# Branch C: the later score stages of one unit placed beside the first score stages of the next unit

## The chip, the cores and the metric

The kernel runs on one core of a Trainium2 chip. The metric is the device time of one execution in microseconds (us); the time of a version is the median over its runs. A core has engines that run side by side, each with its own queue of instructions that it works off in order: the tensor engine (PE; the loading of its weights is listed apart, as PEld), the vector engine (DVE), the scalar engine (ACT), the GpSimd engine (POOL) and the engine whose queue here only starts transfers (SP). They wait for one another through semaphores. Matrix products land in PSUM, in banks of 512 float32 for each of 128 partitions.

## The reference, cut to what matters

One layer of a decoder trunk on 2048 positions with 1024 features. One projection feeds three causal mixers; their gated outputs are joined, multiplied by `w_out`, added to the residual, and normalised:

```python
h = jnp.einsum('bsd,de->bse', x, w_in)
a_u, a_v, a_g, b_val, b_glu, b_g, c_q, c_f, c_i, c_g = jnp.split(h, offsets, axis=-1)
y_a = _sgu_mixer(a_u, a_v, ...) * silu(a_g)          # A: gating over chunks of 128 positions
y_b = _conv_module(b_val, b_glu, ...) * silu(b_g)    # B: causal convolution of width 31
y_c = _hgrn2_mixer(c_q, c_f, c_i, ...) * silu(c_g)   # C: linear recurrence, 4 heads of 128
x = layernorm(ALPHA * x + concat(y_a, y_b, y_c) @ w_out)
```

The change touches branch C alone. Its mixer works on chunks of 64 positions, with `f = lb + (1-lb)*sigmoid(c_f)`, `k = 1-f` and `q = silu(c_q)`:

```python
b = jnp.cumsum(log_f, axis=2)
decay = jnp.exp(jnp.where(causal, b[:, :, :, None, :] - b[:, :, None, :, :], -inf))
scores = jnp.einsum('bhtd,bhsd,bhtsd->bhts', qc, kc, decay)
o_intra = jnp.einsum('bhts,bhsv->bhtv', scores, vc)
o_inter = jnp.einsum('bhtd,bhdv->bhtv', qc * jnp.exp(b), state)
new_state = exp(b_last) * state + einsum('bhsd,bhsv->bhdv', kc * exp(b_last - b), vc)
o = o * rsqrt(mean(o*o) + eps) * norm_g
```

Everything is float32.

## The kernel before, in words

The 2048 positions are four groups of 512, two groups to a half. Each half runs branch B's projections, in the first half branch A as well, then branch C's values, and then eight *units* of branch C: four heads, each with the two groups of the half. After both halves comes the product with `w_out`, and the normalisation. In the profile shown below the eight units of the first half are executed from 219 to 365 us, those of the second half from 519 to 730 us, each with the work left over at its end.

A product of two float32 matrices is written as three matrix instructions (`three`, L200 to L203): each factor is split into a high and a low part, and high by high, high by low and low by high are summed. One such instruction has a 128x128 weight tile and 512 columns. They make up most of the tensor engine's time, and here they are called **stream matmuls**. A unit (`hgrn_unit`, L357 to L583) has three projections of 24 stream matmuls each: `pm_f` (the gate f), `pm_q` (the query) and `pm_cg` (the output gate). Everything else that the unit does on the tensor engine is small work between stream matmuls, its own or those of the next unit:

- stage 0 (L405): 16 matmuls with weight tiles 128x32 and 80 columns, the scores within blocks of 4 positions
- stage 1 (L405): 16 matmuls, 128x32 and 48 columns, blocks of 16
- stage 2 (L440): 8 matmuls, 128x64 and 96 columns, blocks of 64
- the chunk halves (`chunk_halves`, L500): 4 matmuls, 128x64 and 64 columns, blocks of 128
- `transposes` (pk, L515), `states` (pst, L531: four matmuls; after each the vector engine folds the result into the running state, s, L535/L537), `outputs` (po, L549/L553: two matmuls for each of four chunks) and `finish` (pt, L571)

A group of such small matmuls is called a **burst** here. The profile counts each small float32 matmul as two instructions (x32 for 16 of them).

Between the stages the vector engine masks the scores into ST (by way of a buffer S32 for stages 0 and 1, L417 and L423) and prepares the next stage's operand: X1, then X4, X16 and Q64, with the products of f kept in T, and K overwritten stage by stage. ACT copies S32 and the chunk halves into ST (L433, L503), makes KT from pk (L518), takes the squares of the outputs (jk, L558), and applies the sigmoid and silu (f L362, X L369, sg L582). sigmoid, and the others, need different function tables, so that ACT has a table load at changes between them (ACT_TABLE_LOAD).

**What sets the order.** The program counts a virtual clock: each group of three stream matmuls advances it by 0.64 (`tick`, L186). A step of a unit is put into a queue with a due time (`later(dt, fn)`, L182) and is issued at the first tick that reaches it. The distances are the constants in one line: DST0 (unit's projections of f and q to stage 0) 4.5, DST (from each score stage to the next) 5.5, DKT 2.5, DPST 2.0, DPO 2.5, DPT 6.0. So stage 0 of a unit falls near the end of its `pm_cg`, and the later stages fall into the next two units' projections. The compiler's scheduler then places the instructions on each engine; only the small matmuls are kept in their mutual program order (`pinned`), and everything else may move by its dependencies.

Buffers that bear on the order: the projections share three PSUM banks, the score stages two (`sc`), pst, po and the pair pk/pt one each (`st`, `o`, `tr`); K has two buffers, X1, X4, X16 and Q64 one each, sg two, and S32 is one buffer for all units.

Of the kernel before, what the change touches and what calls it, by code (L numbers as in the profile page):

```python
# [27 lines left out]
GPH = NG // NHALF  # L28
# [15 lines left out]
NWARM = 9  # L44
FIRST = ("00", "x0", "x1", "10", "x2", "01", "x3", "x4", "11", "x5", "x6", "x7")
DTAP, DNORM, DWO = (1.5, 1.35), 8.0, 2.5
DST0, DST, DKT, DPST, DPO, DPT = 4.5, 5.5, 2.5, 2.0, 2.5, 6.0


def _masks():  # L50
# [34 lines left out]
def _body(tc, nc, d, ctx):  # L85
    from contextlib import ExitStack

    def pool(name, bufs=1, space=None, stack=ctx, **kw):
        if space is not None:
            kw["space"] = space  # L90
        return stack.enter_context(tc.tile_pool(name=name, bufs=bufs, **kw))
# [90 lines left out]
    def later(dt, fn):  # L182
        heapq.heappush(queue, (clock[0] + dt, order[0], fn))
        order[0] += 1
# [169 lines left out]
                    tick(0.64)  # L354
                nc.scalar.copy(vh[:, gi * 4 + tt, :], pt)  # L355

    def hgrn_unit(h, g, gi, w, x, pl, vh, ST, S32):  # L357
        nm = f"{h}_{g}"
        wf_, wq, wg = w
        pf = proj_f(wf_, x, f"f{nm}")  # L360
# [15 lines left out]
        def tb(ap, *shape):  # L376
            return ap.unsqueeze(len(ap.shape)).to_broadcast(shape)

        def prep(st):
# [6 lines left out]
            else:  # L386
                nc.vector.tensor_mul(X[:, :, 2:6:3, :], X[:, :, 4:7:2, :],
                                     tb(T[:, :, 1:3], P, n, 2, b))
                nc.vector.tensor_mul(X[:, :, 3, :], X[:, :, 5, :], tb(T[:, :, 1], P, n, b))

        def stage(st):
            b = 4 ** st
            n = G // (4 * b)
            nsc = 10 if st == 0 else 6
# [89 lines left out]
            cur["X"], cur["T"] = X, T  # L484
            if st < 2:
                prep(st + 1)
                later(DST, lambda: stage(st + 1))
            else:
                later(DST, chunk_halves)

        def chunk_halves():
            X, T = cur["X"], cur["T"]
# [158 lines left out]
    def getx(g):  # L651
        if g not in xg:
            xg[g] = load_x(g)
        return xg[g]
# [81 lines left out]
    vh = vhp.tile([P, GPH * 4, 512], F32, name="vh")  # L736
# [9 lines left out]
    for hf in range(NHALF):  # L746
        last = hf == NHALF - 1
# [6 lines left out]
        xs = [getx(hf * GPH + gi) for gi in range(GPH)]  # L754
        if hf == 0:
# [3 lines left out]
            with ExitStack() as esw:  # L759
                wo_start(pool("wos", stack=esw, reuse_waits="tile"))  # L760
                with ExitStack() as esa:
                    pl = pool(f"a{hf}", stack=esa, reuse_waits="tile")
# [8 lines left out]
        pl = pool(f"c{hf}", stack=esc, reuse_waits="tile")  # L771
        STs = []
# [4 lines left out]
        S32 = pl.tile([P, 4, 32], F32, name=f"S32{hf}")  # L777
        nc.gpsimd.memset(S32, 0.0)
        u = 0
        for h in range(4):  # L780
            w = [load_wf(o + h, hf) for o in (C_F, C_Q, C_G)]
            for gi in range(GPH):
                hgrn_unit(h, hf * GPH + gi, gi, w, xs[gi], pl, vh, STs[u % 2], S32)
                u += 1
                if h == 3 and gi == 0 and not last:
                    getx(hf * GPH + gi + GPH)
# [83 lines left out]
    with ExitStack() as esa:  # L870
        pl = pool("a1", stack=esa, side="right", reuse_waits="tile")
# [177 lines left out]
```

## Time and profile before

| | |
|---|---|
| median of 3 runs | 933.75 us (932.08 to 935.57) |
| the profiled execution's own time | 934.35 us |
| its span (first to last instruction) | 932.6 us |
| PE matmul busy | 906.8 us, 97% of the span |
| DVE busy | 714.4 us, 77% |
| ACT busy | 392.9 us, 42% |
| POOL busy | 82.1 us, 9% |
| granted TensorE clock, mean | 0.996 |

Busy time of PE is modelled at its ends, and instructions overlap there: two matmuls that start 0.23 us apart are listed with 0.39 us each. What an instruction costs is therefore read from the distance between the starts of its neighbours and not from its listed duration. A row of the timeline gives the start in us, the listed duration, the engine, the line, the operation, output and inputs, the shape, and how many instructions were taken together. Where an engine stood idle before the row, the end of the row names the idle time and what ended it.

### The profile page before, as it was taken

What the parts mean: (1) busy time and instruction counts of PE and PEld (TensorE: products, weight loads), DVE (VectorE), ACT (ScalarE), POOL (GpSimd) and SP (SyncE); (2) the same over time, 40 slices, a digit from 0 to 9 for tenths busy, and PEclk for the clock granted to TensorE, in tenths of its full rate; (3) what the DMA queues carried; (4) which work ended last, traced back from release to release, by engine and by line L of the source; (5) the groups of instructions that cost most, each with busy time, mean ns of one, the idle gap of its engine ahead of it and who ended that gap; (6) DMA issues with size and microseconds to landing.
All of it is one profiled execution on the core that took longest, in us unless ns stands there. A gap on an engine that the chain in (4) does not pass through costs nothing.

```text
span 932.6 us, 15037 instructions
## 1 busy us (share of the span) xinstructions
PE 906.8 (97%) x5673; PEld 735.1 (79%) x5673; DVE 714.4 (77%) x1614; ACT 392.9 (42%) x774; POOL 82.1 (9%) x127
## 2 busy tenths in 40 slices
PE   9999998999999999999999999999999999999996
PEld 6889886787777777788888877777788887888885
DVE  5998889935787768997999767778785144888777
ACT  6524455143345346634314344443553342543350
POOL 0001100000000000101000000001012000221122
PEclk9999999999999999999999999999999999999998
DMA  7516786121112103511202111111151498455422
GB/s 261 180 35 233 251 301 232 46 91 35 34 35 79 35 13 120 165 66 58 68 1 91 45 46 47 47 46 46 50 167 58 145 351 294 159 171 186 139 91 90
DMA packets 60808, 107.43 MB, mean 115 GB/s; under 512 B 5312, under 2 KB 21952, under 8 KB 60608
## 3 DMA queue, kind: packets, MB, share of 16 engines
q1 hardware_dynamic: 60736, 106.48, 33.6%
q8 instruction: 44, 0.72, 0.3%
q14 instruction: 28, 0.23, 0.1%
HBM read 75.00 MB, written 31.46 MB: 114 GB/s over the span
## 4 chain that ended last, share of the span: by engine, by line
PE 65%; DVE 17%; DMA 6%; ACT 4%; issue 4%; POOL 2%; SPq 0%; POOLq 0%; DVEq 0%; ACTq 0%
DVE acc L285 5%; PE pm_q L201 3%; PE poz L201 3%; PE pm_ci L203 3%; PE pm_ci L201 3%; PE pm_ci L202 3%; PE poz L203 3%; PE poz L202 3%; PE pm_q L203 3%; PE pm_q L202 3%; PE pm_f L201 3%; PE pm_f L203 2%; PE pm_f L202 2%; PE pm_cg L201 2%; PE pm_cg L203 2%
## 5 line engine op out<-in xcount | busy, mean ns | idle before, releaser
L285 DVE SCALAR_TENSOR_TENSOR acc<-bh,vec,acc 128x512 f32<-128x512 f32 x240 | 172.2, 752 | 2.6
L148 DVE TENSOR_TENSOR wl<-rw,wh 128x512 fp32r<-128x512 f32 x84 | 56.8, 688 | 25.8 <-ACT wh L147 25.6
L147 ACT CAST wh<-rw 128x512 fp32r<-128x512 f32 x84 | 49.9, 619 | 40.4 <-PE pm_f L202 11.1
L558 ACT ACTIVATE jk<-po 128x128 f32<-128x128 f32 x64 | 17.8, 278 | 58.5 <-PE po L553 57.6
L201 PE MATMUL pm_f<-xhix,wh 128*128 128x512 f32 x96 | 41.1, 429 | 0.0
L201 PE MATMUL pm_q<-xhix,wh 128*128 128x512 f32 x96 | 41.0, 427 | 0.0
L201 PE MATMUL pm_cg<-xhix,wh 128*128 128x512 f32 x96 | 39.0, 407 | 0.0
L202 PE MATMUL pm_q<-xlox,wh 128*128 128x512 f32 x96 | 39.0, 406 | 0.0
L203 PE MATMUL pm_f<-xhix,wl 128*128 128x512 f32 x96 | 37.8, 393 | 0.0
L203 PE MATMUL pm_q<-xhix,wl 128*128 128x512 f32 x96 | 37.8, 393 | 0.0
L202 PE MATMUL pm_f<-xlox,wh 128*128 128x512 f32 x96 | 37.6, 392 | 0.0
L203 PE MATMUL pm_cg<-xhix,wl 128*128 128x512 f32 x96 | 37.6, 391 | 0.0
L202 PE MATMUL pm_cg<-xlox,wh 128*128 128x512 f32 x96 | 37.5, 390 | 0.0
L201 PE MATMUL pm_ci<-wh_ci,xhix 128*128 128x512 f32 x96 | 37.3, 389 | 0.0
L202 PE MATMUL pm_ci<-wl_ci,xhix 128*128 128x512 f32 x96 | 37.3, 389 | 0.0
L203 PE MATMUL pm_ci<-wh_ci,xlox 128*128 128x512 f32 x96 | 37.3, 389 | 0.0
L227 POOL TENSOR_SCALAR crs<-ss 128x4 f32<-128x4 f32 x16 | 4.6, 286 | 371.0 <-ACT jk L558 371.0
L355 ACT COPY vh<-pm_ci 128x512 f32<-128x512 f32 x16 | 9.4, 589 | 58.1 <-PE pm_ci L203 58.1
L446 DVE COPY_PREDICATED ST<-msk,sc 64x192 f32<-64x192 int32 (+2 forms) x96 | 28.7, 299 | 4.9 <-PE sc L440 2.6
L537 DVE SCALAR_TENSOR_TENSOR s<-s,Tc,pst 128x128 f32<-128x128 f32 x56 | 19.4, 346 | 16.1 <-PE pst L531 15.9
L531 PEld LDWEIGHTS pst<-vh,KT 128*128 128x128 f32 x120 | 19.4, 188 | 14.5 <-DVE s L537 10.4
L503 ACT COPY ST<-sc 64x128 f32<-64x128 f32 x32 | 8.4, 261 | 50.9 <-PE sc L500 50.7
(355 smaller groups left out, 2772.0 us busy)
## 6 DMA issues: line engine op xcount, KB each, us to landing
rw<-wf SPq DMA_DIRECT2D x84, 256.0 KB, 3.1
wob<-wo_dr SPq DMA_DIRECT2D x14, 1024.0 KB, 11.5
xr<-x SPq DMA_DIRECT2D x16, 512.0 KB, 3.9
ry<-y_dr SPq DMA_DIRECT2D x32, 256.0 KB, 2.7
out<-xr SPq DMA_DIRECT2D x15, 512.0 KB, 2.6
wo_dr<-wsh SPq DMA_DIRECT2D x28, 256.0 KB, 3.3
wo_dr<-wsl SPq DMA_DIRECT2D x28, 256.0 KB, 2.8
rx<-xT SPq DMA_DIRECT2D x24, 256.0 KB, 3.4
```

The costliest lines, as they stand in the source:

```text
L147: nc.scalar.copy(hi, src)
L148: nc.vector.tensor_sub(lo, src, hi.bitcast(F32))
L201: nc.tensor.matmul(out, wh, xh, start=first, stop=False, **kw)
L202: nc.tensor.matmul(out, wh, xl, start=False, stop=False, **kw)
L203: nc.tensor.matmul(out, wl, xh, start=False, stop=last, **kw)
L285: nc.vector.scalar_tensor_tensor(a, h[:, k : k + G], vcol(cw + k), a, ALU.mult, ALU.add)
L355: nc.scalar.copy(vh[:, gi * 4 + tt, :], pt)
L446: nc.vector.copy_predicated(ST[rr, :, 64 * m + j0 * b : 64 * m + (j0 + nj) * b], msk[rr, mo : mo + mw].unsqueeze(1).to_broadcast([64, 4, mw]),
L503: nc.scalar.copy(ST[0:64, e:4:2, 64:128], pcv[64 * e : 64 * e + 64])
L531: pinned(nc.tensor.matmul(pst[:, cs], KT_[:, cs], V[:, c, :], start=True, stop=True))
L537: nc.vector.scalar_tensor_tensor(ns, stt[-1], Tc[:, c : c + 1], pst[:, cs], ALU.mult, ALU.add)
L558: nc.scalar.activation(jk, po[:, c * P : (c + 1) * P], AF.Square, accum_out=ss[:, c : c + 1])
```

## The change

A new constant DSTH = 7.7 and a dictionary `held` are added, and each unit is told whether it is the last of its half (`u == 7`). After stage 0, stage 1 is due 7.7 later instead of 5.5. Stage 2 and the chunk halves are not put into the queue at all: they are kept in `held`, and the next unit takes them out. Its stage 0 first runs the stage 2 of the unit before; its stage 1 first runs the chunk halves of the unit before. The last unit of a half keeps the old distances for its own steps. Everything that follows the chunk halves (pk, pst, po, pt) keeps its distance to them.

```diff
-DST0, DST, DKT, DPST, DPO, DPT = 4.5, 5.5, 2.5, 2.0, 2.5, 6.0
+DST0, DST, DSTH, DKT, DPST, DPO, DPT = 4.5, 5.5, 7.7, 2.5, 2.0, 2.5, 6.0
...
+    held = {}
+
+    def hgrn_unit(h, g, gi, w, x, pl, vh, ST, S32, last):
...
+        def then(st, fn):
+            if last:
+                later(DST, fn)
+            elif st == 1:
+                later(DSTH, fn)
+            else:
+                held[st - 2] = fn
+
         def stage(st):
+            if st < 2 and st in held:
+                held.pop(st)()
             b = 4 ** st
...
             if st < 2:
                 prep(st + 1)
-                later(DST, lambda: stage(st + 1))
+                then(st + 1, lambda: stage(st + 1))
             else:
-                later(DST, chunk_halves)
+                then(3, chunk_halves)
...
-                hgrn_unit(h, hf * GPH + gi, gi, w, xs[gi], pl, vh, STs[u % 2], S32)
+                hgrn_unit(h, hf * GPH + gi, gi, w, xs[gi], pl, vh, STs[u % 2], S32, u == 7)
```

From the second of these places on, the line numbers are 3 to 13 higher in the changed kernel: L405 becomes L418, L440 L453, L500 L513, L515 L528, L531 L544, L571 L584, and L582 L595.

How the instructions stand on the engines: in the names, the two numbers after sc, pk, pst and the like are head and group, so that `1_1` is one unit of the first half and `2_0` the next one; `sc` has the stage as third number, 3 being the chunk halves. The first place is the tensor engine, from the `pm_cg` of unit 2_0 to the states of unit 1_1. Before:

```order
L440 MATMUL sc1_1_2_2965<-X16_1_1_2872,K1_1_2541 64x96 x8
...
L405 MATMUL sc2_0_0_3006<-X12_0_2952,K2_0_2841 32x80 x16
...
L571 MATMUL pt1_0_3045<-ident_91,os1_0_2944 128x128 x4
...
L500 MATMUL sc1_1_3_3058<-Q64_1_1_2980,K1_1_2541 64x64 x4
...
L515 MATMUL pk1_1_3081<-ident_91,K1_1_2541 128x128 x4
...
L405 MATMUL sc2_0_1_3100<-X4_2_0_3027,K2_0_2841 32x48 x16
...
L531 MATMUL pst1_1_3142<-vh_113,KT1_1_3086 128x128
```

And in the changed kernel:

```order
L453 MATMUL sc1_1_2_2958<-X16_1_1_2877,K1_1_2516 64x96 x8
L418 MATMUL sc2_0_0_2981<-X12_0_2907,K2_0_2816 32x80 x16
...
L562 MATMUL po1_0_3020<-vh_113,ST0_0_1843 128x128 x2
...
L584 MATMUL pt1_0_3081<-ident_91,os1_0_3040 128x128 x4
...
L513 MATMUL sc1_1_3_3094<-Q64_1_1_2973,K1_1_2516 64x64 x4
L418 MATMUL sc2_0_1_3105<-X4_2_0_3002,K2_0_2816 32x48 x16
...
L528 MATMUL pk1_1_3160<-ident_91,K1_1_2516 128x128 x4
...
L544 MATMUL pst1_1_3179<-vh_113,KT1_1_3165 128x128
```

Stream matmuls stand at each "...". Stage 2 of unit 1_1 and stage 0 of unit 2_0, which had 18 stream matmuls between them, are neighbours, and so are the chunk halves of 1_1 and stage 1 of 2_0. The pk of unit 1_1 now stands 12 stream matmuls behind the second pair, 3 into the `pm_cg` of unit 2_1, and its first pst 12 further on; the pt of unit 1_0 stands 9 stream matmuls into the `pm_q` of unit 2_1, where it stood 3 into `pm_f`. In each half 14 pairs come about in this way, 28 in all, and no pair has a stream matmul between its parts.

The second place is the vector engine around the states of unit 1_1 (s, four instructions), before:

```order
L423 COPY_PREDICATED S320_1847<-msk_97,sc2_0_1_3100 128x8x4
L364 TENSOR_SCALAR f2_1_3091<-f2_1_3091,oml_106,lb_105 128x512
L537 SCALAR_TENSOR_TENSOR s1_1_0_3144<-s1_0_3_2901,Tc1_1_3067,pst1_1_3142 128x128
L365 TENSOR_SCALAR K2_1_3093<-f2_1_3091 128x512
L148 TENSOR_TENSOR wl_27_0_3306<-rw27_0_1_3311,wh_27_0_3305 128x512
L537 SCALAR_TENSOR_TENSOR s1_1_1_3147<-s1_1_0_3144,Tc1_1_3067,pst1_1_3142 128x128
...
L371 TENSOR_TENSOR X12_1_3196<-X12_1_3196,f2_1_3091 128x128x2
```

And in the changed kernel:

```order
L436 COPY_PREDICATED S320_1847<-msk_97,sc2_0_1_3105 128x8x4
L368 TENSOR_SCALAR K2_1_3068<-f2_1_3066 128x512
L374 TENSOR_TENSOR X12_1_3150<-X12_1_3150,f2_1_3066 128x128x2
L375 TENSOR_TENSOR X12_1_3150<-X12_1_3150,f2_1_3066 128x128x2
L470 COPY X4_2_1_3245<-X12_1_3150 128x32x2 x2
L387 TENSOR_TENSOR X12_1_3150<-X12_1_3150,f2_1_3066 128x128x2
L388 TENSOR_TENSOR X12_1_3150<-X12_1_3150,f2_1_3066 128x128
L482 TENSOR_TENSOR f2_1_3066<-f2_1_3066 128x128
L550 SCALAR_TENSOR_TENSOR s1_1_0_3181<-s1_0_3_2947,Tc1_1_3103,pst1_1_3179 128x128
L471 TENSOR_TENSOR X4_2_1_3245<-X12_1_3150,f2_1_3066 128x32x2x3 x2
L550 SCALAR_TENSOR_TENSOR s1_1_1_3184<-s1_1_0_3181,Tc1_1_3103,pst1_1_3179 128x128
```

The four s of unit 1_1 stood ahead of the preparation of X1 for unit 2_1; now the first of them stands behind six rows of that preparation.

The third place is ACT over the same stretch, before:

```order
L503 COPY ST0_1_1845<-sc1_1_3_3058 64x2x64 x2
L582 ACTIVATE sg2_0_3039<-pm_cg2_0_2958 128x512
L518 COPY KT1_1_3086<-pk1_1_3081 128x512
L147 CAST wh_27_0_3305<-rw27_0_0_3307 128x512
L362 ACT_TABLE_LOAD
L362 ACTIVATE f2_1_3091<-pm_f2_1_3041 128x512
...
L433 COPY ST0_0_1843<-S320_1847 32x4x32 x4
...
L369 ACTIVATE X12_1_3196<-pm_q2_1_3096 128x128x4
```

And in the changed kernel:

```order
L365 ACT_TABLE_LOAD
L365 ACTIVATE f2_1_3066<-pm_f2_1_3016 128x512
L147 CAST wh_27_0_3279<-rw27_0_1_3285 128x512
L516 COPY ST0_1_1845<-sc1_1_3_3094 64x2x64 x2
L446 COPY ST0_0_1843<-S320_1847 32x4x32
L595 ACT_TABLE_LOAD
L595 ACTIVATE sg2_0_3014<-pm_cg2_0_2913 128x512
L446 COPY ST0_0_1843<-S320_1847 32x4x32 x3
L372 ACTIVATE X12_1_3150<-pm_q2_1_3071 128x128x4
L531 COPY KT1_1_3165<-pk1_1_3160 128x512
```

Between the chunk halves' copy and the X1 of the next unit ACT now has a copy out of S32, a table load, the sg of unit 2_0, and three more copies, and KT follows X1 where it stood ahead of f. It stands so only in units during which weights are cast; elsewhere the four copies out of S32 stand together.

More of the change, by code (lines that the diff above doesn't have):

```diff
@@ L355, in values @@
                 nc.scalar.copy(vh[:, gi * 4 + tt, :], pt)
-    def hgrn_unit(h, g, gi, w, x, pl, vh, ST, S32):
+    held = {}
+    def hgrn_unit(h, g, gi, w, x, pl, vh, ST, S32, last):
         nm = f"{h}_{g}"
```

## The prediction

> **What bounds the kernel now.** I read the page first: busy time, and the chain that ended last.
>
> ```profile
> span 932.6 us, 15037 instructions
> PE 906.8 (97%) x5673; PEld 735.1 (79%) x5673; DVE 714.4 (77%) x1614; ACT 392.9 (42%) x774; POOL 82.1 (9%) x127
> PE 65%; DVE 17%; DMA 6%; ACT 4%; issue 4%; POOL 2%; SPq 0%; POOLq 0%; DVEq 0%; ACTq 0%
> ```
>
> The tensor engine is busy for 97% of the span. The chain runs through other engines for a third of the span, but they lead it only where a late operand happens to be the last thing that PE asked for. So the time is the sum of PE's steps plus the short waits between them, and the change can act in two ways: on the price of a step between two kinds of matmul, and on waits for a late operand. I then read a long piece of the second half's units by window (busy time and count of PE, PEld, DVE, ACT, POOL; granted clock; DMA share; GB/s).
>
> ```profile
> 502.00:628.00 126.00, 125.77 (x982) 99.69 (x980) 93.55 (x293) 55.23 (x123) 6.57 (x10) 1.00 0.17 57
> ```
>
> DVE is at 74% and ACT at 44% while PE has hardly a gap: both have slack on average, not at every place. The clock is 1.00, so it is no term.
>
> **The price of a burst.** The timeline of PE, at stage 2 of one unit and, 18 stream matmuls later, stage 0 of the next, the pair that the change puts together:
>
> ```profile
> 603.56 0.39 PE L202 MATMUL pm_cg<-xlox,wh 128*128 128x512 f32 x1
> 603.79 0.39 PE L203 MATMUL pm_cg<-xhix,wl 128*128 128x512 f32 x1
> 604.11 0.88 PE L440 MATMUL sc<-X,K 128*64 128x96 f32 x16
> 604.91 0.50 PE L201 MATMUL pm_cg<-xhix,wh 128*128 128x512 f32 x1
> 605.25 0.40 PE L202 MATMUL pm_cg<-xlox,wh 128*128 128x512 f32 x1
> ...
> 608.90 0.39 PE L203 MATMUL pm_cg<-xhix,wl 128*128 128x512 f32 x1
> 609.22 0.76 PE L405 MATMUL sc<-X,K 128*32 128x80 f32 x32
> 609.91 0.50 PE L201 MATMUL pm_f<-xhix,wh 128*128 128x512 f32 x1
> ```
>
> A stream matmul follows another after 0.23 (603.56 to 603.79). The step from a stream matmul into a burst is 0.32 (603.79 to 604.11; 608.90 to 609.22): 0.09 too much. The burst itself, up to the start of the next stream matmul, is 0.80 and 0.69. The step after that first stream matmul is again slow, 0.34 (604.91 to 605.25): 0.11 too much. What a merged pair costs turns on one step that this kernel never makes, from a 64-row burst to a 32-row burst. The nearest rows are a place where a burst is followed by another kind of burst, and, for later, stage 1 with the stream behind it:
>
> ```profile
> 258.42 0.76 PE L405 MATMUL sc<-X,K 128*32 128x80 f32 x32
> 259.11 0.66 PE L316 MATMUL bt<-ident,acc 128*128 128x128 f32 x4
> ...
> 668.49 0.55 PE L405 MATMUL sc<-X,K 128*32 128x48 f32 x32
> 668.97 0.50 PE L201 MATMUL pm_q<-xhix,wh 128*128 128x512 f32 x1
> ```
>
> At 258.42 the follower, a transposition, starts 0.69 after the burst's start, to the hundredth when a stream matmul starts behind the same burst (609.22 to 609.91). So I take it that the second burst of a pair starts where the stream matmul would have started, and that a pair saves one way out and one way in: 0.11 + 0.09 = 0.20. Bounds for the unknown step: the 64-row burst takes 0.80 for 8 matmuls, by the single starts in the trace some 0.63 of it up to the start of its last one (0.09 each) and 0.17 from there to the follower. If a follower of another shape cost no more than another of its own kind, the step would be 0.09, and the pair would save 0.08 more, 0.28. If it cost what the way in from a stream matmul costs, 0.32, the pair would save 0.15 less, 0.05.
>
> [...]
>
> 28 pairs at 0.20 are 5.6 us (7.8 and 1.4 at the bounds). Against it, the new order breaks 8 small bursts apart, with a po, pst or pt next to another kind of burst or to a stream matmul between; each costs one such step more, 8 x 0.20 = 1.6. **Net of the steps: -4.0** (-6.2 to +0.2). Nothing is added or removed besides: the matmuls, the masks, the table loads and the DMAs are the same in number. The transfers have slack: the DMA share of the window is 0.17.
>
> **The waits that branch C causes now.** The view of waits of PE (engine, line, what it waited for; us, times, longest):
>
> ```profile
> PE pst L531 <- DVE s L537: 2.7, 5, 0.9
> PE pk L515 <- DVE K L505: 2.3, 2, 1.5
> ...
> PE bt L316 <- ACT os L563: 1.2, 1, 1.2
> ...
> PE pst L531 <- DVE bhn L324: 0.8, 1, 0.8
> PE bb L330 <- DVE sg L573: 0.7, 1, 0.7
> ...
> PE pst L531 <- DVE s L535: 0.3, 1, 0.3
> ```
>
> Together 8.0 us in 11 waits. Such a row counts from the modelled end of the matmul before, so it is a little short:
>
> ```profile
> 596.90 0.39 PE L201 MATMUL pm_q<-xhix,wh 128*128 128x512 f32 x1
> 597.52 0.49 PE L531 MATMUL pst<-vh,KT 128*128 128x128 f32 x2 [0.23 <-DVE s L537]
> ...
> 598.55 0.39 PE L531 MATMUL pst<-vh,KT 128*128 128x128 f32 x2
> 599.48 0.39 PE L531 MATMUL pst<-vh,KT 128*128 128x128 f32 x2
> ```
>
> The distance is 0.62 where 0.23 is normal: 0.39 lost, not the 0.23 of the row's end. With 0.16 more for each of 11 I take 9.8 us now. Of these, 4.3 lie in the leftovers of the last units behind the two halves: the longest pk wait, 1.5, the one behind s L535, 0.3, and three of the five behind s L537, 1.7 together, with 5 x 0.16.
>
> **The waits afterwards.** pst has one bank and a chain: a pst waits until s has read the one before. pst are pinned among the small matmuls, but the stream stands behind them in PE's order, so a late s stops everything. In the new order the first s stands behind the preparation of the next unit's X1, which waits for the silu on ACT (X), and that behind the copies into ST, a table load and sg. I lay this out from the start of the second pair (chunk halves and stage 1) as zero.
>
> PE: the pair takes 0.86 (0.23 for the chunk halves up to the start of the last and 0.15 from there to the follower, by single starts, 0.48 for stage 1 as at 668.49, where the stream goes on at 668.97); 12 stream matmuls with one slow step bring pk to 3.7; pk (0.5) and 12 more bring the first pst to 6.9; the second is due 0.93 later as between 598.55 and 599.48, at 7.8.
>
> ACT and DVE, with the durations of these rows (ACT, then DVE):
>
> ```profile
> 589.31 0.53 ACT L503 COPY ST<-sc 64x128 f32<-64x128 f32 x2 [2.90 <-PE sc L500]
> 593.08 0.60 ACT L582 ACTIVATE sg<-pm_cg 128x512 f32<-128x512 f32 x1 [3.24 <-DMA y_dr<-sg]
> 594.17 1.28 ACT L362 ACT_TABLE_LOAD   x1
> 597.25 1.22 ACT L433 COPY ST<-S 32x128 f32<-32x128 f32 x4 [1.18 <-DVE S L423]
> 604.41 0.67 ACT L369 ACTIVATE X<-pm_q 128x512 f32<-128x512 f32 x1
> ```
>
> ```profile
> 597.12 0.34 DVE L537 SCALAR_TENSOR_TENSOR s<-s,Tc,pst 128x128 f32<-128x128 f32 x1
> ...
> 605.11 0.48 DVE L371 TENSOR_TENSOR X<-X,f 128x256 f32<-128x256 f32 x1 [2.27 <-ACT X L369]
> 605.50 0.52 DVE L372 TENSOR_TENSOR X<-X,f 128x256 f32<-128x256 f32 x1
> 606.14 0.57 DVE L384 TENSOR_TENSOR X<-X,f 128x256 f32<-128x256 f32 x1
> 607.15 0.40 DVE L385 TENSOR_TENSOR X<-X,f 128x128 f32<-128x128 f32 x1
> 610.03 0.39 DVE L469 TENSOR_TENSOR f<-f 128x128 f32<-128x128 f32 x1
> ...
> 614.31 0.42 DVE L504 TENSOR_TENSOR Q<-Q,T 128x256 f32<-128x256 f32 x1
> 614.64 0.42 DVE L505 TENSOR_TENSOR K<-K,T 128x256 f32<-128x256 f32 x1
> ```
>
> The chunk halves are copied by 1.0. The first copy out of S32 waits for the masks of stage 1. DVE does Q and K of the chunk halves ahead of them, 0.33 each by the starts at 614.31 and 614.64, and K of stage 1 between them; with about 0.4 for the first scores to arrive and 1.2 for three masks and that K, my estimate is 2.3. Then 0.31 for the copy, 1.28 for the table, 0.60, 0.92 for three copies and 0.67 for the silu: X is ready at 6.1. DVE then takes, by the distances of such rows, about 0.4 + 0.4 + 0.2 (the copy into X4) + 0.6 + 0.4 + 0.3 = 2.3 up to the start of the first s, and the second pst can start 0.4 after that (597.12 to 597.52 at the wait above): X's end plus 2.7. Due at 7.8, it is late if X ends later than 5.1. KT follows X on ACT and is ready at 6.7, just before the first pst.
>
> So a unit with a copy ahead of the table load (weights are cast there) is late by 1.0. In a unit without, table load and sg run while the masks are made, X ends at about 4.9, and the lateness is nothing to 0.2; I take 0.1. Seven units of each half run with a merged predecessor: the first of each half, with its queue fuller, 1.0 each; three with casts, 3.0; seven light ones, 0.7; one in the first half in which the transposes of the convolution's norm fall into the same banks (bank `o` and `st`, the waits of bt and bb above), 3.0; and the last of the first half, where two casts stand ahead of the table load, 2.2. Sum 10.9. The leftovers fall from 4.3 to 2.6, since pk's wait (1.5 + 0.16) goes: pk stands 12 matmuls behind the pair there. 13.5 against 9.8: **+3.7**. Bounds: all light and no collision, 14 x 0.1 + 2.6 = 4.0, which is -5.8; all late by 1.1 with both collisions (1.9 and 1.1 more) and unchanged leftovers, 15.4 + 3.0 + 4.3 = 22.7, +12.9.
>
> The other steps that move wait for nothing new: sg's projection shares its bank with a projection two thirds of a unit later, and the last pt of each half stands where it stood, so that loads that wait for the units' end do not move.
>
> **The sum.** -4.0 + 3.7 = -0.3 on the profiled execution's 934.35. That one lies 0.6 above the median of 933.75, so I predict **933.5 us**, which is no change that can be told (I call 0.5%, 4.7 us, the least that can).
>
> **Rivals.**
>
> *The waits do not grow.* The pairs save their 4.0, and the units' waits go down to some 3 (14 x 0.2) besides the leftovers' 2.6: 5.6 against 9.8, -4.0 - 4.2 = -8.2, 925.5. For it: DVE is free a quarter of the time, ACT over half, and the scheduler may have ordered by better times than my addition. Against it: the six rows ahead of the first s are in the order whatever the times, and X waits for `pm_q`'s end. 0.29.
>
> *The chain X, X1, s becomes the bound of every unit.* If X ends later than 5.1 in all 14 units, each pays 1.1, and with collisions the waits are 22.7: -4.0 + 12.9 = +8.9, 942.7. It decides from 5.1 on; the light units are 0.2 below that, the others 1.0 above. A table load of 1.28 more in one unit's ACT order is enough. For it: the margin is small, and the s rows of one unit hold four chances to be late. Against it: a lateness of the first pst lets DVE catch up for the following ones. 0.18.
>
> *The step from 64 to 32 rows costs what the way in costs.* Then the pairs save 28 x 0.05 = 1.4, less than the 1.6 of the broken bursts, and nothing pays for the waits: +3.9, 937.7. For it: every way into a burst from stream matmuls in the rows above is 0.32. Against it: 258.42. 0.09. [...]
>
> *That it does not do what it says* is out: the order has the 28 pairs as neighbours.
>
> **How the numbers follow.** No measurable change 0.44, waits do not grow 0.29, chain 0.18, full step 0.09. The likeliest alone spans 929.1 to 938.4. The range takes in the first rival's price and most of the second's: 925 to 942. Faster by over 0.5%: 0.29. Slower by over 0.5%: the chain and a third of the last, 0.21. The rest, 0.50, within 0.5%.
>
> **What would show it.** Right: in the timeline of PE the second burst of a pair starts about 0.80 (stage 2) or 0.38 (chunk halves) after the first, and the stream goes on with one slow step; in the view of waits pst behind s grows from 2.7 to about 7, with the units with casts and the first of each half as its largest. Wrong: a distance in the pair of 0.64 + 0.32; or s rows that start before X1's rows need them, with pst waits as now (then faster); or pst waits of one us in every unit (then slower). A new wait of pk for K or of the stream for a bank would be one that I have not seen.

## The result and the profile after

The changed kernel takes 941.39 us (median of 6 runs, 940.46 to 942.31), the kernel before 933.36 on the same chip: a ratio of 1.008 with a 95% interval of 1.0069 to 1.0091. It is 8.0 us slower. The predicted time was 933.5 us, no change; the rival "the chain X, X1, s becomes the bound of every unit" had 942.7. The profiled execution's span is 940.6 us, also 8.0 us longer than before. From the page:

```profile
span 940.6 us, 15020 instructions
PE 908.7 (97%) x5673; PEld 740.7 (79%) x5673; DVE 715.4 (76%) x1614; ACT 394.0 (42%) x774; POOL 80.5 (9%) x127
```

The counts of instructions on the engines are those of before, and so is nearly all busy time. The time went into gaps. The view of waits of PE, over the stretch of branch C's units and what follows them (219 to 730 us; the first unit's projections start at 200 already, and there is no such wait between 200 and 219):

```profile
PE pst L544 <- DVE s L550: 6.4, 11, 1.2
PE pk L528 <- DVE sg L586: 1.9, 2, 1.4
PE pst L544 <- ACT KT L531: 1.6, 2, 1.3
PE pst L544 <- DVE s L548: 1.3, 2, 0.7
PE pt L584 <- ACT os L576: 1.1, 1, 1.1
PE pm_av L201 <- ACT vg L625: 1.1, 1, 1.1
PE po L562 <- DVE bhn L324: 1.0, 1, 1.0
PE bb L330 <- ACT KT L531: 0.8, 1, 0.8
```

Behind s (L550, L548 here) pst waited 3.0 us in 6 places before and waits 7.7 us in 13 now. pk behind sg, pst behind KT and `pm_av` behind vg are new. The rows with pt, po and bb are meetings with the transpositions of the convolution's norm, of which there were three before (bt, pst behind bhn, and bb), and pk's wait for K of before, 2.3 us, is gone. For a sum I again use the distances of the starts: every step of PE above 0.36 us between 200 and 760 us counts with what it has above a normal 0.235. Before, that is 9.7 us in 12 places; after, 19.8 us in 30.

**The pairs themselves came out as priced.** The timeline of PE at the second and then the first kind of pair:

```profile
625.39 0.45 PE L513 MATMUL sc<-Q,K 128*64 128x64 f32 x8
625.77 0.55 PE L418 MATMUL sc<-X,K 128*32 128x48 f32 x32
626.25 0.50 PE L201 MATMUL pm_q<-xhix,wh 128*128 128x512 f32 x1
...
636.58 0.47 PE L203 MATMUL pm_cg<-xhix,wl 128*128 128x512 f32 x1
636.99 0.88 PE L453 MATMUL sc<-X,K 128*64 128x96 f32 x16
637.80 0.76 PE L418 MATMUL sc<-X,K 128*32 128x80 f32 x32
638.49 0.50 PE L201 MATMUL pm_f<-xhix,wh 128*128 128x512 f32 x1
638.83 0.39 PE L202 MATMUL pm_f<-xlox,wh 128*128 128x512 f32 x1
```

From stage 2 to stage 0 it is 0.81, as it was 0.80 from stage 2 to a stream matmul; from stage 0 to the stream 0.69 as before, and one slow step (638.49 to 638.83) behind both instead of one behind each. The way from a 64-row burst into a 32-row burst costs what the way out costs, not the 0.32 of the way in. With the median price of each kind of step in the two traces, the changed order is 3.4 us cheaper between the first unit and the end of the second half's leftover; everything above those prices is 11.7 us dearer there; together +8.3. (By the prices of the kernel before alone, as in the table at the end of the experiments, the order is 4.2 us cheaper.)

**Where the waits come from.** One unit of the second half with a weight cast, on ACT, DVE and PE; its second pair starts at 625.39:

```profile
627.68 0.30 ACT L446 COPY ST<-S 32x128 f32<-32x128 f32 x1 [1.26 <-DVE S L436]
627.99 1.28 ACT L595 ACT_TABLE_LOAD   x1
629.28 0.60 ACT L595 ACTIVATE sg<-pm_cg 128x512 f32<-128x512 f32 x1
629.89 0.91 ACT L446 COPY ST<-S 32x128 f32<-32x128 f32 x3
630.83 0.67 ACT L372 ACTIVATE X<-pm_q 128x512 f32<-128x512 f32 x1
```

```profile
631.53 0.48 DVE L374 TENSOR_TENSOR X<-X,f 128x256 f32<-128x256 f32 x1 [1.48 <-ACT X L372]
631.93 0.52 DVE L375 TENSOR_TENSOR X<-X,f 128x256 f32<-128x256 f32 x1
...
633.49 0.35 DVE L388 TENSOR_TENSOR X<-X,f 128x128 f32<-128x128 f32 x1
...
633.87 0.30 DVE L550 SCALAR_TENSOR_TENSOR s<-s,Tc,pst 128x128 f32<-128x128 f32 x1
```

```profile
632.65 0.38 PE L544 MATMUL pst<-vh,KT 128*128 128x128 f32 x2
...
633.34 0.40 PE L203 MATMUL pm_cg<-xhix,wl 128*128 128x512 f32 x1
634.22 0.49 PE L544 MATMUL pst<-vh,KT 128*128 128x128 f32 x2 [0.48 <-DVE s L550]
```

X is ready 6.1 us after the pair's start, s starts at 8.5, the second pst at 8.8. The step from the stream matmul to that pst takes 0.88 instead of 0.235. Behind the waiting pst stands the stream of `pm_cg`, so PE stops. Of the eight rows between X and s only four belong to X1; the other four, of 0.15 to 0.40 us each, are the convolution's norm, which has no part in the prediction's sum for such a unit.

### The profile page after: what moved, and what is told of

The parts are those of the page before. It is cut to its first block, busy times and chain, and to the rows that moved or that the text cites. A ratio compares the mean times of both kernels' runs of the same rounds, so it can differ in the third digit from the quotient of the medians.

```text
span 940.6 us, 15020 instructions
## 1 busy us (share of the span) xinstructions
PE 908.7 (97%) x5673; PEld 740.7 (79%) x5673; DVE 715.4 (76%) x1614; ACT 394.0 (42%) x774; POOL 80.5 (9%) x127
## 4 chain that ended last, share of the span: by engine, by line
PE 63%; DVE 18%; ACT 6%; DMA 5%; issue 4%; POOL 3%; SPq 0%; POOLq 0%; DVEq 0%; ACTq 0%
DVE acc L285 5%; PE poz L201 3%; PE poz L203 3%; PE poz L202 3%; PE pm_ci L201 3%; PE pm_f L201 3%; PE pm_ci L203 3%; PE pm_ci L202 3%; PE pm_f L203 3%; PE pm_f L202 3%; PE pm_q L201 2%; PE pm_q L202 2%; PE pm_q L203 2%; PE pst L544 2%; PE pm_cg L203 1%
## 5 line engine op out<-in xcount | busy, mean ns | idle before, releaser
L148 DVE TENSOR_TENSOR wl<-rw,wh 128x512 fp32r<-128x512 f32 x84 | 56.4, 686 | 22.9 <-ACT wh L147 22.7
L571 ACT ACTIVATE jk<-po 128x128 f32<-128x128 f32 x64 | 17.8, 278 | 91.0 <-PE po L566 89.6
L201 PE MATMUL pm_f<-xhix,wh 128*128 128x512 f32 x96 | 39.2, 408 | 0.0
L544 PEld LDWEIGHTS pst<-vh,KT 128*128 128x128 f32 x120 | 19.7, 193 | 22.9 <-DVE s L550 15.3
L544 PE MATMUL pst<-vh,KT 128*128 128x128 f32 x120 | 26.7, 305 | 9.3 <-DVE s L550 6.4
L576 ACT ACTIVATE os<-po,crs 128x128 f32<-128x128 f32 x64 | 18.3, 369 | 26.1 <-POOL crs L228 26.1
```

The lines of the kernel that those rows point to most:

```text
L148: nc.vector.tensor_sub(lo, src, hi.bitcast(F32))
L201: nc.tensor.matmul(out, wh, xh, start=first, stop=False, **kw)
L544: pinned(nc.tensor.matmul(pst[:, cs], KT_[:, cs], V[:, c, :], start=True, stop=True))
L571: nc.scalar.activation(jk, po[:, c * P : (c + 1) * P], AF.Square, accum_out=ss[:, c : c + 1])
L576: nc.scalar.mul(os_[:, c * P : (c + 1) * P], po[:, c * P : (c + 1) * P], rs[:, c : c + 1])
```

## The experiments

Two theories stood against each other at first. **W**: the pairs save their steps, and the loss lies in waits for steps that the change makes late. **M**: putting bursts together saves nothing or does the harm itself. All medians are of runs beside runs of the kernel before on the same chip; the ratio is to those, and a difference between two kernels is that of their differences to the kernel before. The runs are called e1 to e12, in the order in which they are told.

### No pairs, the same delays

```diff
             if st < 2 and st in held:
-                held.pop(st)()
+                later(1.28, held.pop(st))
```

> The changed kernel with the same delays but no pairs: the held stage 2 (or chunk halves) comes two ticks, some 10 stream matmuls, behind the next unit's stage 0 (or stage 1) and not beside it. Theory W (the pairs save their steps, the loss is in waits for steps that now come late): the order's steps cost 5.8 us more than the changed kernel's, priced by the step durations of the trace, and the waits stay: 941.4 + 5.8 = 947, give or take 2. Rival M (putting two bursts together saves nothing, or itself makes the masks and copies behind them late): 941 or less.

Measured (e1): 949.9 us (948.9 to 950.76), ratio 1.0167 (1.0154 to 1.018), against 1.008 for the changed kernel: 8 us slower than with the pairs. M falls: it had 941 or less. W had 947 give or take 2 and is short by 1 to 3 us. The held stage stands 6 to 9 stream matmuls behind the next unit's stage in the trace, not 10. pst's waits behind s grow:

```profile
PE pst L544 <- DVE s L550: 10.0, 11, 2.0
```

But other waits shrink along, and by the distances of the starts the sum of the waits stays at 19.7 us, so the waits are not what W is short by. The steps are: by the median prices of all the traces here, and not of before alone, this order costs some 7 us more than the changed kernel's, which would give about 948.6.

### The four pst together

```diff
             for c in range(nst):
                 cs = slice(c * P, (c + 1) * P)
                 pinned(nc.tensor.matmul(pst[:, cs], KT_[:, cs], V[:, c, :], start=True, stop=True))
+            for c in range(nst):
+                cs = slice(c * P, (c + 1) * P)
                 ns = stp.tile(...)
```

The four products go to four quarters of one bank, so that none needs the s of the one before. First on the changed kernel:

> The changed kernel with the four pst matmuls of a unit issued together and the four s on the vector engine behind them, so that no pst waits for an s. Theory W: the pst waits behind s, 10.7 us by the distances of the starts, go, and 1.3 us of steps with them: 929 to 932. Rival Q (the vector engine is simply too late with the unit's work, so that the stop moves to the next matmul that needs s or a bank): 938 or more, with new waits at po, pk or the score stages.

Measured (e2): 934.92 us, ratio 0.9998 (0.9983 to 1.0013). Its 12 runs spread wider than those of the other kernels, from 929.63 to 937.51; the last section comes back to that. The 7.2 us gained against the changed kernel are most of what the pst waits behind s were worth, and not one such wait is left in its view of waits (219 to 760 us), which begins:

```profile
PE pk L528 <- DVE sg L588: 5.2, 3, 3.1
PE bb L330 <- ACT KT L531: 2.2, 1, 2.2
PE pst L544 <- ACT KT L531: 1.9, 3, 1.3
PE po L564 <- DVE bhn L324: 1.2, 1, 1.2
```

It misses the expected 929 to 932, because others grew: pk behind sg went from 1.9 to 5.2 us, and the granted clock fell twice (0.50 from 649 to 651 us; 0.55 and 0.59 in the two stretches of 2 us from 716 on). The same on the kernel before:

> The kernel before with the same regrouping of pst and s. Theory W: its pst waits behind s are 5.0 us and the steps 0.4, so 933.4 - 5.4 = 928. With e2 it tells what the pairs are worth when pst doesn't wait: by theory W e2 minus e3 is the steps, -5, and the other new waits, +4 to +8, so -1 to +3. Rival M: e2 stays 8 us above e3.

Measured (e3): 928.31 us (927.27 to 928.96), ratio 0.9935 (0.9923 to 0.9947). The 928 of the expectation was met. But the difference of e2 and e3 is 6.6 us where -1 to +3 was expected: with pst out of the way, the change still loses nearly as much. So the waits behind s were not the whole of it.

### The last two units as before

```diff
-                hgrn_unit(..., S32, u == 7)
+                hgrn_unit(..., S32, u >= 6)
```

> The changed kernel, but the last two units of a half keep the old distances, so that nothing is held over into the last unit: 12 pairs a half and not 14. If the leftovers of the two halves lost what their places in the trace say (the seventh handover and what follows it, 6 to 8 us with the pk that waits for sg): 934 to 937. If every handover loses the same (8 us over 14): 941.4 - 1.1 = 940.

Measured (e4): 938.64 us (937.02 to 939.02), ratio 1.0042 (1.003 to 1.0054): 3.5 us better than the changed kernel. That is less than the leftovers' share was put at, and three times an even share: the last handover of each half costs more than the others, and does not hold the whole loss.

### The pairs without the extra delay

```diff
-            if last:
+            if last or st != 2:
                 later(DST, fn)
-            elif st == 1:
-                later(DSTH, fn)
             else:
-                held[st - 2] = fn
+                held[0] = fn
```

Only stage 2 is held over here. Stage 1 and the chunk halves are then both due 5.5 behind the first pair, so that they become the second pair by themselves, 27 stream matmuls behind the first and not 39, by the traces.

> The changed kernel with stage 1 due 5.5 after stage 0 as before, and not 7.7; only stage 2 is held over, and the chunk halves come 5.5 behind it. Since both distances are then 5.5, both pairs still come about (the order has 28 pairs), but the second pair and all steps behind it stand 18 stream matmuls, 4 us, nearer to the first. The steps cost 1.3 us less than the changed kernel's. If the loss were the lateness of the later steps as such, the time falls to 934 or less. Theory W as refined: what counts is where s stands on the vector engine against the preparation of X1. There s now stands behind the first rows of it, while X itself is ready 0.7 to 1 us later counted from the second pair, so pst still waits about 1 us a unit: 938 to 941.

Measured (e5): 933.38 us (931.67 to 934.21), ratio 0.9992 (0.9983 to 1.0002). The expectation of W as refined, 938 to 941, was wrong. The loss is gone with the extra delay; what is left of a gain lies within the interval. The vector engine of this kernel, in one unit of the second half:

```profile
576.90 0.47 DVE L374 TENSOR_TENSOR X<-X,f 128x256 f32<-128x256 f32 x1
577.29 0.52 DVE L375 TENSOR_TENSOR X<-X,f 128x256 f32<-128x256 f32 x1
577.67 0.34 DVE L548 SCALAR_TENSOR_TENSOR s<-s,Tc,pst 128x128 f32<-128x128 f32 x1
```

Two rows of X1's preparation stand ahead of the first s, 0.8 us, where six stand in the changed kernel's order at the place shown before the prediction (and the eight rows, 2.3 us, from 631.53 to 633.87 in the unit above). The pair is 12 stream matmuls nearer than in the changed kernel, not the 18 of the expectation. X is later against it, as expected: it ends 7.1 to 8.3 us after the pair's start in nine of the ten units that have an X there, against 5.1 to 6.7 in eleven of twelve in the changed kernel. But in those nine just two rows stand between X and s, and in the changed kernel six to eleven. The nearer place of s weighs more, and the pst behind s wait less:

```profile
PE pst L542 <- DVE s L548: 1.4, 3, 0.8
```

With the four pst together:

> e5 with the four pst together as in e2. Theory W: no wait for s is left on the tensor engine; steps 5.7 us below those of e3 (928.3), other new waits between 0 and 5 us: 923 to 928. Rival Q (the later steps of a unit collide elsewhere whatever their distance): 932 to 936, as e2.

Measured (e6): 925.24 us (923.36 to 926.58), ratio 0.9902 (0.9886 to 0.9918), within the expectation of W. It is about 3 us below e3, which has the same grouping and no pairs; what the pairs alone are worth is asked with e9.

### pk in the bank of pst

```diff
-            pk = bank("tr", 1, f"pk{nm}")
+            pk = bank("st", 1, f"pk{nm}")
```

On e2. pk and pt share the bank `tr`; the vector engine's sg has to read pt before pk may be written.

> e2 with pk moved from the bank that it shares with pt to the bank of pst, which needs the copy of pk anyway. In e2 pk waited in four places of the two leftovers until the vector engine had read pt (sg), 5.8 us together by the distances of the starts, and the clock fell behind the longest, about 1 us. If these waits are that bank's: 928 to 930. If the leftovers are late whatever the bank (the vector engine has too much to do there): 933 or more.

Measured (e7): 926.1 us (924.89 to 928.76), ratio 0.9918 (0.9902 to 0.9934), 2 us better than expected and 8.5 us below e2. What e2 still lost against e3 was mostly this one bank; e7's trace has neither of the two falls of the clock that e2's has (mean clock 0.993 against 0.989). The same wait in the changed kernel, in the second leftover, PE and then DVE:

```profile
721.04 0.60 PE L584 MATMUL pt<-ident,os 128*128 128x128 f32 x4
724.02 0.55 PE L528 MATMUL pk<-ident,K 128*128 128x128 f32 x3 [1.43 <-DVE sg L586]
```

```profile
722.76 0.41 DVE L631 TENSOR_SCALAR vhat<-vg,amv,ars 128x256 f32<-128x256 f32 x1 [0.95 <-POOL ars L228]
723.21 0.75 DVE L586 SCALAR_TENSOR_TENSOR sg<-pt,vec,sg 128x512 f32<-128x512 f32 x1
```

sg stands behind vhat of branch A, whose second half follows the units there, and vhat waits for POOL. pt is done at 721.6, sg reads it at 723.2, and pk, due 1.4 us earlier, goes at 724.0. On e6 the same edit:

> e6 with pk in the bank of pst, as in e7. In e6 one pk waited for the vector engine's reading of pt, 1.4 us beyond a normal step. If that is the bank: 923 to 925. If the second leftover is late whatever the bank: 925 to 927, as e6.

Measured (e8): 923.35 us (923.05 to 923.93), ratio 0.9886 (0.9872 to 0.9901), as expected if it is the bank. It beats both kernels, the one before by 10.6 us. What PE still waits for most in it:

```profile
PE pst L542 <- ACT KT L529: 3.6, 3, 1.9
PE po L562 <- DVE bhn L324: 1.0, 1, 1.0
```

### What the pairs are worth where no pst waits for s

e6 with `later(1.28, held.pop(st))` as in the first experiment.

> e6 with the held stage 2 two ticks, some 10 stream matmuls, behind the next unit's stage 0, so that neither pair comes about. What 28 pairs are worth where no pst waits for s. Theory W: the order's steps cost 5.4 us more than those of e6, so 925.2 + 5.4 = 930.6, between 929 and 933. Rival M (pairs save nothing): 926 or less.

Measured (e9): 927.5 us (925.7 to 928.48), ratio 0.9926 (0.991 to 0.9941): 2.1 us slower than e6 and not 5.4, below the range of W and above that of M, and the intervals of the two ratios overlap. By the distances of the starts e6 waits 8.5 us and this kernel 4.3. In the views of waits pst waits 3.4 us behind KT in e6 and 0.4 here, pk 1.4 us behind sg there and never here, and bt and bb, 1.6 us together, don't wait here at all. So the edit moves the waits as well as the steps, and no run shows what the 28 pairs are worth alone. Against e8, where pk has left pt's bank and whose interval lies apart, e9 is 4.2 us slower; e9 still has the shared bank, but no pk waits for sg in it.

### The delay alone

```diff
-            if last:
+            if last or st != 1:
                 later(DST, fn)
-            elif st == 1:
-                later(DSTH, fn)
             else:
-                held[st - 2] = fn
+                later(DSTH, fn)
```

> The kernel before with the one constant changed, stage 1 due 7.7 after stage 0, nothing held over and no pair. Steps +0.4 us by their prices; the states come 12 stream matmuls later, and zero to two rows of the preparation of X1 stand ahead of the first s, as in e5, where the wait was some 0.2 us a unit: 934 to 938. If any delay of the later steps costs as the change's does (8 us for some 36 stream matmuls): 936 to 937 as well, so that it doesn't tell the two apart; it tells whether the constant alone could have been the loss, 941 or more.

Measured (e10): 935.82 us (934.03 to 936.78), ratio 1.0014 (1.0003 to 1.0025). The constant by itself is not the loss. Holding over alone (e5) costs nothing, the constant alone 1.9 us, and both together 8.0. In the traces the chunk halves stand 81 stream matmuls behind stage 0 before, 93 here, 99 in e5 and 111 in the changed kernel, 30 later than before and not the 36 of the expectation. The constant costs where holding over has already put the steps back: with both, s comes behind the whole preparation of X1.

### The unit's output not over sg

In the changed kernel's trace the units without a cast show another wait. In the one whose second pair starts at 601.64, on ACT:

```profile
603.54 1.28 ACT L595 ACT_TABLE_LOAD   x1 [0.87 <-DMA y_dr<-sg]
604.84 0.60 ACT L595 ACTIVATE sg<-pm_cg 128x512 f32<-128x512 f32 x1
605.33 1.21 ACT L446 COPY ST<-S 32x128 f32<-32x128 f32 x4
606.56 0.69 ACT L372 ACTIVATE X<-pm_q 128x512 f32<-128x512 f32 x1
```

sg has two buffers, and `finish` multiplies into sg and stores it. With pt later, the store of the unit before last lands only at 603.5, and table load, sg, copies and X queue up behind it: X ends at 5.6 after the pair. This edit writes the product over os instead:

```diff
-            nc.vector.scalar_tensor_tensor(sg, pt, vcol(V_NG + h), sg, ALU.mult, ALU.mult)
-            y_store(4 + h, g, sg)
+            nc.vector.scalar_tensor_tensor(os_, pt, vcol(V_NG + h), sg, ALU.mult, ALU.mult)
+            y_store(4 + h, g, os_)
```

> The changed kernel with the unit's last product written over os and stored from there, not over sg. The trace of the changed kernel shows table load and sg on ACT waiting in five places until the store of the unit before last, which goes out from the same one of two sg buffers, has landed (5.1 us); the finish, and so the store, comes later by the change. Here that wait cannot arise, and sg stands ahead of the copies into ST. If the late store is what makes X late in the units without a cast: X ends at 4.2 to 4.9 after the second pair, the waits of pst behind s fall from 7.7 to some 3 us, and the fall of the clock in the first half's last unit goes: 934 to 937. If the place of s behind the preparation of X1 is enough for the waits by itself: 939 to 941.

Measured (e11): 945.62 us (944.71 to 947.38), ratio 1.013 (1.0109 to 1.0151), 3.6 us *slower* than the changed kernel. X does end at 4.2 in most units of the second half, as expected, and the waits of pst behind s grow to 12.0 us all the same:

```profile
PE pst L544 <- DVE s L550: 9.3, 11, 1.4
PE pst L544 <- DVE s L548: 2.7, 3, 1.0
```

The vector engine shows why, in the unit whose second pair starts at 603.47:

```profile
607.71 0.49 DVE L374 TENSOR_TENSOR X<-X,f 128x256 f32<-128x256 f32 x1 [1.98 <-ACT X L372]
...
611.52 0.42 DVE L390 TENSOR_TENSOR X<-X,T 128x256 f32<-128x256 f32 x1
611.98 0.29 DVE L392 TENSOR_TENSOR X<-X,T 128x128 f32<-128x128 f32 x1
612.19 0.34 DVE L550 SCALAR_TENSOR_TENSOR s<-s,Tc,pst 128x128 f32<-128x128 f32 x1
```

The order now has the whole preparation of X1 and a part of X4's ahead of the first s, twelve rows with the K of the unit among them, 4.5 us. That the scheduler placed s so because X comes earlier in its plan is likely and not shown. s starts at X's end plus the rows ahead of it: 4.2 + 4.5 here, 6.1 + 2.4 in the unit of the changed kernel shown above, 7.1 + 0.8 in four units of e5. So X's end alone does not make s late, and the place that s gets in the vector engine's order counts as much; both expectations were wrong, the one that went by X more so. Where pst does not wait for s, the same edit is worth a lot:

> e8 with the same edit. Its largest remaining waits are pst behind KT, 3.6 us in three places. If these hang on the store too: 920.5 to 922.5. If not: 922.5 to 924.

Measured (e12): 917.08 us (916.38 to 918.53), ratio 0.9824 (0.9804 to 0.9845), 6.3 us below e8 and 3.4 below the expected range. In e8 ACT waits for the landing of such a store in seven places, 8.8 us; here in none, and pst's wait behind KT, 3.6 us, is gone with it. This is the fastest version found, 1.8% below the kernel before. Not all of the 6.3 us is shown to come from the edit: in the two traces, 7.0 us apart, the units, up to the product with `w_out`, are 3.9 us shorter, and another 3.1 us lie ahead of the first unit, where both have the same instructions in the same order (200 us in before, 202.0 in e8, 198.9 here).

### All together

The steps, priced from the order of each kernel with the step durations of the trace of before; the waits, as the sum described above; and both against before, beside the measured difference (us):

| kernel | steps | waits | steps + waits against before | measured |
|---|---|---|---|---|
| before | 0 | 9.7 | 0 | 0 |
| changed | -4.2 | 19.8 | +5.9 | +8.0 |
| e1 no pairs, same delays | +1.6 | 19.7 | +11.6 | +15.8 |
| e2 changed, pst together | -5.5 | 15.5 | +0.3 | +0.8 |
| e3 before, pst together | -0.4 | 5.8 | -4.3 | -5.8 |
| e4 last two units plain | -3.8 | 16.3 | +2.8 | +4.6 |
| e5 no extra delay | -5.5 | 11.0 | -4.2 | -0.5 |
| e6 e5, pst together | -6.1 | 8.5 | -7.3 | -8.6 |
| e7 e2, pk elsewhere | -5.5 | 7.5 | -7.7 | -7.7 |
| e8 e6, pk elsewhere | -6.1 | 6.5 | -9.3 | -10.6 |
| e9 e6 without pairs | -0.8 | 4.3 | -6.2 | -6.5 |
| e10 delay alone | +0.4 | 9.2 | -0.1 | +1.9 |
| e11 changed, output over os | -4.0 | 22.7 | +9.0 | +11.6 |
| e12 e8, output over os | -6.2 | 3.0 | -12.9 | -16.9 |

The two columns order the kernels rightly but for two of them that move by one or two places (e7 and e10), and miss single ones by up to 4.2 us; waits under 0.13 us each are in neither. Two things besides are in neither. Ahead of the first unit all these traces have the same instructions in the same order on every engine, and yet the first unit starts anywhere from 198.8 (e6) to 202.0 us (e8): a single profiled execution can be off by as much. And the step from the first to the second instruction of a pst takes 0.21 instead of 0.12 in 34 of 60 places of e5, in 29 of the changed kernel and in 13 before. Of the 3.7 us by which the columns miss e5, its trace shows 2.0 in such short steps and 0.9 in a later start of the first unit; 0.8 stay open.

## Why the prediction was wrong, point by point

**The frame held.** The time is PE's steps plus its waits, and the change acts on both. The waits of before were put at 9.8 us; by the distances of the starts they are 9.7.

**The steps held.** 0.20 a pair was taken, with 0.28 and 0.05 as bounds for the unknown step. The rows at 636.99 and 637.80 show the way out that was taken, and -4.0 for the order is -3.4 by the prices of both traces. All 28 pairs have this step: counted from the start of the first burst's last instruction it is 0.18 behind stage 2 and 0.15 behind the chunk halves, where the longest steps inside these two bursts, but for their first, are 0.08 and 0.05. The rival of the full step is out. Behind these bursts the change of the tile's shape cost the same whether the next tile was 128x32 or 128x128: in the changed kernel it is 0.18 behind stage 2 in the 14 pairs and in the seven places where a 128x128 tile follows, and 0.15 behind the chunk halves in the 14 pairs and in the four such places, 0.10 us above those longest steps.

**The step that failed is the term for the waits: +3.7 us, 13.5 against 9.8, where the traces show +10.1, 19.8 against 9.7.** The ledger for a unit with a cast came out to a tenth in the unit shown: pk at 3.7, the first copy at 2.3, X at 6.1, the second pst at 8.8. The last of these is partly luck, since a transposition of the convolution's norm puts the first pst there at 7.3 and not 6.9, and four small rows of that norm take the place of X1's other rows ahead of s. Three steps of the term were wrong.

First, the sentence "In a unit without, table load and sg run while the masks are made, X ends at about 4.9, and the lateness is nothing to 0.2". Table load and sg wait for a store there (603.54 above), X ends at 5.6, and the pst is 0.7 late. That store wait is one that the prediction had excluded with "The other steps that move wait for nothing new": in the view of before it stood in plain sight, with ACT idle anyway, and the change moved pt, and so the store, up to the place where X hangs on it. The pst of the units with no collision wait 0.7 to 1.0 us nearly throughout, only two have 0.1 and 0.3. But e11 and e5 show that the reasoning from X's end alone was not enough: with X at 4.2 the waits are longer, with X at 7.1 shorter. What has to be read is how many rows the order puts ahead of s. The order shown before the prediction gave six for one unit; the ledger took their durations for all units and then asked only when X arrives. The convolution's norm meets pst in the second half too (1.4 and 1.5 us in two units there), which was counted for the first half alone. Units in all: 14.5 us where 10.9 was taken.

Second, "The leftovers fall from 4.3 to 2.6, since pk's wait goes". That wait did go. A new one came in its place, for pk and pt, which share a bank, now stand so near that pk is due 1.5 us behind pt's start, at 721.04 above; e7 shows what it is worth when pst no longer hides it. With the `pm_av` behind vg, leftovers are 4.3 us.

Third, the clock. It was left out as no term, on the 1.00 of the window of before. The windows of the changed kernel in the last unit of the first half:

```profile
377.41:380.83 3.42, 1.74 (x8) 1.23 (x9) 3.39 (x12) 0.40 (x1) 0.00 (x0) 1.00 0.41 139
380.83:384.24 3.41, 3.41 (x14) 2.71 (x14) 2.13 (x8) 0.62 (x2) 0.00 (x0) 0.50 0.00 0
```

After two waits of 1.5 and 1.4 us PE runs at half clock for 3.4 us, and its steps from one stream matmul to the next take 0.42 to 0.57 there: 1.1 us more. This is the profiled execution, with a mean clock of 0.991; the other five runs of the changed kernel have 0.994 and are 0.5 to 1.9 us faster, so the fall may be missing in them, and the median may hold nothing of it.

**The rivals.** The one that was taken as the third likeliest is what happened in place and size: pst waits for an s behind X1's preparation in nearly every unit. Its condition, X later than 5.1, is met in all twelve units that have an X there (5.1 to 7.9), but it is not what decides (e5, e11). Its 8.9 against 8.0 is partly luck: it has 1.1 for each of 14 units, and neither the clock nor pk's bank. What spoke for it, that the margin is small, should have weighed more, since the lateness of a light unit was a difference of two sums of some 8 us each, taken to 0.1. What spoke for "the waits do not grow", that the scheduler may order by better times, did not come: in the changed kernel six to eleven rows stand between X and s, and in e11, with an earlier X, still more.

## What to carry to other kernels

A burst of small matmuls cost 0.09 us on its way in (0.32 against 0.23) and 0.11 on its way out (0.34 against 0.23) here, and bringing two together saved one of each; but a step that is moved to make that happen takes its whole train along, and each follower's place in the other engines' orders has to be read anew: what stands ahead of its producer there, who shares its bank, and whose store its buffer waits for. Where a chain of matmul and vector operation alternates on one bank, issue the matmuls together if they write different parts of it: that gave more here (5.8 us in e3) than the change was after (4.0 us of steps by the forecast). And where a forecast is a small difference of long queues on two engines, take the rival that needs only a little more lateness as seriously as the forecast.

## What the runs showed of the hardware that was not expected

The granted clock fell to 0.5 without a long idle time: behind steps of 1.70 and 1.62 us with three stream matmuls between them in the changed kernel, and behind one step of 2.55 us, from 645.48, in e2. It did not fall behind one of 1.86 us in the kernel before or of 2.46 us in e5. The traces show what tells them apart. While PE has work, every fall lasts 3.41 us or twice that, and within a trace the falls and returns lie a whole number of 3.41 us apart: in the changed kernel the falls start at 155.55, 165.79 and 380.83 us, 3 and 63 times 3.413 apart. If each trace is cut into stretches on this grid, the stretch ahead of the changed kernel's fall (377.41 to 380.83, shown above) holds its second wait and the end of the first, and the one ahead of e2's fall holds nearly all of its wait, while e5's wait is cut in two by an edge at 371.89. The stretch ahead of the fall in e2, and e5's stretch with most of its wait (the number behind the comma is the busy time of PE, the third from the end the clock):

```profile
644.53:647.94 3.41, 1.34 (x6) 0.75 (x4) 0.39 (x2) 3.34 (x7) 0.00 (x0) 1.00 0.00 0
368.48:371.89 3.41, 1.78 (x8) 1.13 (x6) 2.67 (x9) 3.14 (x7) 0.00 (x0) 1.00 0.42 144
```

Between 172 and 760 us the fourteen traces have four falls: two in e2 and one each in e1 and the changed kernel. PE, as the profile models it, is busy for 0.13, 0.39, 0.36 and 0.51 of the stretch ahead of them. No other stretch has less than the 0.52 of e5, and none of them is followed by a fall. Ahead of 172 us the border is less sharp: in the kernel before a stretch with 0.46 (159.93 to 163.35) has no fall behind it, the next one, with 0.48, has. So the stretch ahead of a fall was not always an idle one: in the changed kernel PE was busy for 0.51 of it. Such falls in some runs and not in others would also fit the spread of e2: its four fastest runs, up to 931.8 us, have a mean clock of 0.991 to 0.994, the seven from 934.8 us on 0.989 to 0.991. Which of its waits met an edge in which run no trace shows.
